# Re-cutting the last step's loads of a row-wise dot product: nine transfers become eight

## The chip, the cores and the metric

The kernel runs on one core of one Trainium2 chip. The time is that of the device for one execution, in microseconds (us). The kernel before takes 320.35 us, the median of three runs (320.31 to 320.41). The engines that matter here are VectorE (called DVE in the profile), ScalarE (ACT), SyncE (SP, which issues most transfers) and the core's 16 DMA engines. TensorE does no work.

## The reference

```
gram = np.matmul(x, y.transpose(0, 2, 1))          # x, y: (8, 4096, 512) float32
diag = np.diagonal(gram, axis1=1, axis2=2)         # (8, 4096)
diag = diag - diag.max(axis=-1, keepdims=True)
exp = np.exp(diag)
return exp / exp.sum(axis=-1, keepdims=True)
```

Only the diagonal of the product is used, so the work is 8 x 4096 dot products of a row of x with the same row of y, 512 long, and then a softmax over the 4096 values of each batch. Each input has 67.1 MB and is read once.

## The kernel before, in words

**Tiling.** Four batches at a time lie on the 128 partitions, 32 partitions to a batch, and each partition holds 128 consecutive rows of one batch (C = 128). The two groups of four batches are i = 0 and i = 1. A step `t` takes 32 of those 128 rows (R = 32) on all partitions, so there are eight steps, four to a group. A step's x is a tile of 128 x 32 x 512 (8.4 MB), its y as well. One "row" below means one row on every partition: 128 x 512 values, 256 KB.

**Buffers.** x has two buffers, `xs[0]` and `xs[1]`, used in turn. y has only one, `ys`. So the load of the next y must wait until the present y has been read. To let it go sooner, ScalarE copies a few rows of y elsewhere, so that VectorE may read these rows from the copy.

**Steps 0 to 5** (lines 123 to 134): load all 32 rows of x and of y, copy the last 6 rows of y to `side`, multiply on VectorE in two instructions (26 rows from `ys`, 6 from `side`, in place in `xs`, line 72), sum 30 rows on VectorE (line 75) and 2 rows on ScalarE (line 80).

**Step 6** (lines 136 to 146) has the same loads, but its y is cut at row F, which is H + 1 = 17. ScalarE copies the L = 9 rows of y that end at F into `spare`, which is rows 23 to 31 of `xs[1]`, the x buffer of step 7 (lines 139 and 140). VectorE multiplies the F - L = 8 rows ahead of these, then the 9 rows from `spare`, then the last 15 rows from `ys` (lines 141 to 143). After the first of the three and ScalarE's copy, rows 0 to 16 of `ys` are free. ScalarE sums 30 of the rows and VectorE 2.

**Step 7** (lines 149 to 161) loads x and y in nine pieces and takes them as they land. After each piece is issued, the rows that then have both x and y (`both`) are given to `dots`: one VectorE instruction a row, which multiplies and sums at once (line 85). The pieces are x 15, y 17, x 8, y 10, x 6, y 3, x 2, y 2, x 1 rows. When `both` reaches F, VectorE takes the largest of the values so far (line 161), 48 of them, and a later instruction on line 99 takes the largest of the remaining 18.

**The order of the work** is written by hand: each engine runs its instructions in program order and waits where a tile that it needs isn't ready. All loads and the first group's output transfers go through SP's queue in that order; an issue that waits holds up all issues behind it. A load waits for the instructions that last read or wrote its own rows of the buffer. The first y piece of step 7 (rows 0 to F - 1) thus waits for ScalarE's copy and VectorE's first product in step 6; the second y piece waits for the third product; an x piece that touches `spare` waits for the second product, which reads it.

**The end** (lines 163 to 169): eight small output transfers of the first group on SP, then the largest value, the exponential on ScalarE, the sum, the reciprocal, the scaling on VectorE, and the second group's output from ScalarE's queue.

Of the kernel before, what the change touches and what calls it, by code (L numbers as in the profile page):

```python
# [1 line left out]

# [5 lines left out]


@with_exitstack
def kernel(
    ctx: ExitStack,
    tc: tile.TileContext,
    x: bass.AP,
    y: bass.AP,
    out: bass.AP,
):
    nc = tc.nc
    ctx.enter_context(tc.manual_schedule())  # L20
    f32 = mybir.dt.float32
    Alu = mybir.AluOpType
    Act = mybir.ActivationFunctionType
    X = mybir.AxisListType.X
    B, N, D = x.shape
    P = nc.NUM_PARTITIONS
    G = 32
    Q = P // G
    C = N // G
    R = 32  # L30
    H = R // 2
    K = 6
    W = 2
    F = H + 1
    L = 9
    S = B // Q * (C // R)


    xv = x.rearrange("(s b) (j c) d -> s (b j) c d", b=Q, j=G)
    yv = y.rearrange("(s b) (j c) d -> s (b j) c d", b=Q, j=G)  # L40
    ov = out.rearrange("(s b) (j c) -> s (b j) c", b=Q, j=G)

    big = ctx.enter_context(tc.tile_pool(name="big", bufs=1))
    small = ctx.enter_context(tc.tile_pool(name="small", bufs=1))


    xs = [big.tile([P, R, D], f32, name=f"xs{i}") for i in range(2)]
    ys = big.tile([P, R, D], f32, name="ys")
    side = big.tile([P, K, D], f32, name="side")

    diag = [small.tile([P, C + 2 * i], f32, name=f"diag{i}") for i in range(B // Q)]
    res = [small.tile([P, C], f32, name=f"res{i}") for i in range(B // Q)]

    def columns(t, r0, n):
        c0 = t % (C // R) * R + r0
        return slice(c0, c0 + n)

    def rows(t, r0, n):
        return xs[t % 2][:, r0 : r0 + n, :]

    def dots_of(t, r0, n):
        return diag[t * R // C][:, columns(t, r0, n)]

    def load_x(t, r0, n):
        nc.sync.dma_start(out=rows(t, r0, n), in_=xv[t * R // C, :, columns(t, r0, n), :])  # L65

    def load_y(t, r0, n):
        nc.sync.dma_start(out=ys[:, r0 : r0 + n, :], in_=yv[t * R // C, :, columns(t, r0, n), :])  # L68

    def products(t, r0, n, yt):  # L70
        xt = rows(t, r0, n)
        nc.vector.tensor_tensor(out=xt, in0=xt, in1=yt, op=Alu.mult)  # L72

    def sums(t, r0, n):
        nc.vector.tensor_reduce(out=dots_of(t, r0, n), in_=rows(t, r0, n), axis=X, op=Alu.add)  # L75

    def sums_act(t, r0, n):
        for r in range(r0, r0 + n):
            row = xs[t % 2][:, r, :]
            nc.scalar.activation(out=row, in_=row, func=Act.Copy, accum_out=dots_of(t, r, 1))  # L80

    def dots(t, r0, n):
        for r in range(r0, r0 + n):
            xt = xs[t % 2][:, r, :]
            nc.vector.scalar_tensor_tensor(  # L85
                out=xt, in0=xt, scalar=1.0, in1=ys[:, r, :], op0=Alu.mult, op1=Alu.mult,
                accum_out=dots_of(t, r, 1),
            )

    def over_quadrant(name, column, op, negate=False):  # L90

        got = small.tile([P, 1], f32, name=name)
        nc.vector.tensor_reduce(  # L93
            out=got, in_=column.to_broadcast([P, G]), axis=X, op=op, negate=negate, apply_transpose=True
        )
        return got

    def largest(out, d):
        nc.vector.tensor_reduce(out=out, in_=d, axis=X, op=Alu.max)  # L99

    def exps(i, d):
        mxp = small.tile([P, 1], f32, name=f"mxp{i}")
        largest(mxp, d)
        nmx = over_quadrant(f"nmx{i}", mxp, Alu.max, negate=True)
        sump = small.tile([P, 1], f32, name=f"sump{i}")
        nc.scalar.activation(out=res[i], in_=diag[i][:, :C], func=Act.Exp, bias=nmx, scale=1.0, accum_out=sump)  # L106
        return sump

    def normalize(i, sump):
        total = over_quadrant(f"sum{i}", sump, Alu.add)  # L110
        rc = small.tile([P, 1], f32, name=f"rc{i}")
        nc.vector.reciprocal(out=rc, in_=total)  # L112
        nc.vector.tensor_single_scalar(out=res[i], in_=res[i], scalar=rc, op=Alu.mult)  # L113

    nc.vector.addr_align(128, offset=0, max_nops=0)
    nc.scalar.addr_align(128, offset=0, max_nops=0)

    nc.sync.drain()  # L120
    nc.sync.drain()  # L121

    for t in range(S - 2):
        load_x(t, 0, R)
        load_y(t, 0, R)
        nc.scalar.activation(out=side, in_=ys[:, R - K :, :], func=Act.Copy)  # L126
        if t == C // R:
            normalize(0, sump)
        products(t, 0, R - K, ys[:, : R - K, :])
        products(t, R - K, K, side)  # L130
        sums(t, 0, R - W)
        sums_act(t, R - W, W)
        if t == C // R - 1:
            sump = exps(0, diag[0])

    t = S - 2
    load_x(t, 0, R)
    load_y(t, 0, R)
    spare = rows(t + 1, R - L, L)
    nc.scalar.activation(out=spare, in_=ys[:, F - L : F, :], func=Act.Copy)  # L140
    products(t, 0, F - L, ys[:, : F - L, :])
    products(t, F - L, L, spare)
    products(t, F, R - F, ys[:, F:, :])
    sums(t, R - W, W)
    sums_act(t, 0, R - W)
    largest(diag[1][:, C + 1 :], diag[1][:, : C - 2 * R])


    t += 1
    upto = {load_x: 0, load_y: 0}  # L150
    done = 0
    for load, n in (
        (load_x, H - 1), (load_y, F), (load_x, 8), (load_y, 10), (load_x, 6), (load_y, 3), (load_x, 2), (load_y, 2), (load_x, 1)
    ):
        load(t, upto[load], n)
        upto[load] += n
        both = min(upto.values())
        dots(t, done, both - done)
        done = both
        if done == F:  # L160
            largest(diag[1][:, C : C + 1], diag[1][:, C - 2 * R : C - R + H])

    met = small.tile([P, C - R], f32, name="met")
    nc.scalar.activation(out=met, in_=diag[1][:, : C - R], func=Act.Copy)  # L164

    for p in range(0, P, H):
        nc.sync.dma_start(out=ov[0, p : p + H, :], in_=res[0][p : p + H, :])
    normalize(1, exps(1, diag[1][:, C - R + H :]))
    nc.scalar.dma_start(out=ov[1], in_=res[1])


# [1 line left out]
_INS = ['x', 'y']  # L173
_OUTS = [((8, 4096), 'float32')]


# [23 lines left out]
```

## Time and profile before

| what | value |
|---|---|
| median of three runs | 320.35 us (320.31 to 320.41) |
| profiled execution, first to last instruction (span) | 318.8 us |
| median less span | 1.55 us |
| VectorE busy | 241.7 us (76%) |
| ScalarE busy | 49.8 us (16%) |
| DMA moved | 134.37 MB, mean 421 GB/s |
| HBM read, written | 134.22 MB, 0.13 MB |

The span runs from the first to the last instruction of one profiled execution. The page gives no other time of that execution; what the measured median has above its span, 1.55 us, lies outside the instructions. Where the trace gives a transfer's "us to landing", it counts from the start of its issue on the queue to the time when all 16 DMA engines have reported it done. A share of DMA above 1 in a very short stretch only says that packets are booked at the moment when they begin. "issue" in the chain is time in which an engine waited for nothing that the profile shows.

### The profile page before, as it was taken

The page shows a single profiled execution, that of the slowest core. Times are in us where ns is not written, and L with a number is a line of the kernel's source. Part 1 is how long each engine was busy: PE and PEld are TensorE (multiplying, and loading weights), DVE is VectorE, ACT ScalarE, POOL GpSimd, SP SyncE. Part 2 cuts the span into 40 slices and gives each one's busy share as a digit, 9 for nine tenths or more (in the row PEclk, how much of TensorE's full clock was granted, in tenths as well). Part 3 has the DMA queues.
Part 4 walks back from the last instruction along what each step waited for, and adds up shares of the span by engine and source line. Part 5 has one row for each costly group of instructions (what it writes and reads, how often), then busy time and mean ns, then how long its engine had stood idle before and what let it go on. Part 6 is the DMA issues. An engine that isn't in the chain of part 4 may idle for free.

```text
span 318.8 us, 315 instructions
## 1 busy us (share of the span) xinstructions
DVE 241.7 (76%) x98; ACT 49.8 (16%) x97; POOL 0.2 (0%) x4
## 2 busy tenths in 40 slices
DVE  0000069995899939999399994999939998599996
ACT  1000030100301003010120103000030100596700
POOL 0000000000000000000000000000000000000000
DMA  9999999999999999999999999999999999999993
GB/s 372 419 395 469 452 395 452 469 395 395 493 428 395 469 452 395 428 477 411 395 485 436 395 469 452 395 403 493 419 395 469 452 395 452 394 440 410 429 411 112
DMA packets 3714, 134.37 MB, mean 421 GB/s; under 512 B 512, under 2 KB 768, under 8 KB 1280
## 3 DMA queue, kind: packets, MB, share of 16 engines
q1 hardware_dynamic: 3568, 134.29, 97.7%
q10 hardware_dynamic: 144, 0.07, 0.1%
q14 instruction: 2, 0.02, 0.0%
HBM read 134.22 MB, written 0.13 MB: 421 GB/s over the span
## 4 chain that ended last, share of the span: by engine, by line
DMA 65%; DVE 33%; SPq 1%; issue 0%; ACT 0%; DVEq 0%
DMA ys<-in_y_dram 65%; DVE xs L72 32%; DVE xs L85 0%; SPq L65 0%; SPq L68 0%; DVE res L113 0%; DVE sum L93 0%; DVE nmx L93 0%; ACT res L106 0%; DVE mxp L99 0%; DVE rc L112 0%; DVEq L72 0%; SPq L121 0%; SPq L120 0%
## 5 line engine op out<-in xcount | busy, mean ns | idle before, releaser
L72 DVE TENSOR_TENSOR xs<-xs,ys 128x13312 f32<-128x13312 f32 (+2 forms) x8 | 96.7, 12091 | 71.9 <-DMA ys<-in_y_dram 71.9
L75 DVE TENSOR_REDUCE diag<-xs 128x30 f32<-128x15360 f32 (+1 forms) x7 | 98.1, 14020 | 0.2
L80 ACT ACTIVATE xs<-xs 128x512 f32<-128x512 f32 x42 | 25.9, 617 | 90.4 <-DVE xs L72 90.4
L126 ACT ACTIVATE side<-ys 128x3072 f32<-128x3072 f32 x6 | 16.6, 2763 | 124.1 <-DMA ys<-in_y_dram 124.1
L85 DVE SCALAR_TENSOR_TENSOR xs<-xs,ys 128x512 f32<-128x512 f32 x32 | 19.9, 687 | 1.1 <-DMA ys<-in_y_dram 1.0
L72 DVE TENSOR_TENSOR xs<-xs,side 128x3072 f32<-128x3072 f32 x6 | 20.1, 3351 | 0.0
L80 ACT ACTIVATION_READ_ACCUMULATOR xs<-xs 128x1 f32 x42 | 7.9, 187 | 0.0
L140 ACT ACTIVATE xs<-ys 128x4608 f32<-128x4608 f32 x1 | 4.0, 4043 | 20.0 <-DMA ys<-in_y_dram 20.0
L106 ACT ACTIVATE res<-diag,nmx 128x128 f32<-128x128 f32 x2 | 0.8, 402 | 30.1 <-DVE nmx L93 30.1
L72 DVE TENSOR_TENSOR xs<-xs,xs 128x4608 f32<-128x4608 f32 x1 | 5.0, 4951 | 0.0
L85 DVE DVE_READ_ACCUMULATOR xs<-xs,ys 128x1 f32 x32 | 2.6, 82 | 0.0
L126 ACT ACT_TABLE_LOAD x1 | 1.3, 1283 | 1.2 <-PEq L184 1.2
L93 DVE TRANSPOSE_TENSOR_REDUCE sum<-sump 128x1 f32<-128x32 f32 x2 | 0.4, 212 | 1.2 <-ACT res L106 1.2
L113 DVE TENSOR_SCALAR res<-res,rc 128x128 f32<-128x128 f32 x2 | 0.6, 286 | 0.1
L99 DVE TENSOR_REDUCE mxp<-diag 128x1 f32<-128x128 f32 (+1 forms) x2 | 0.5, 229 | 0.1
L93 DVE TRANSPOSE_TENSOR_REDUCE nmx<-mxp 128x1 f32<-128x32 f32 x2 | 0.4, 211 | 0.1
L99 DVE TENSOR_REDUCE diag<-diag 128x1 f32<-128x64 f32 (+1 forms) x2 | 0.4, 202 | 0.0
L112 DVE RECIPROCAL rc<-sum 128x1 f32<-128x1 f32 x2 | 0.3, 164 | 0.1
L106 ACT ACTIVATION_READ_ACCUMULATOR res<-diag,nmx 128x1 f32 x2 | 0.4, 186 | 0.0
L164 ACT ACTIVATE met<-diag 128x96 f32<-128x96 f32 x1 | 0.3, 283 | 0.0
L184 POOL MEMSET const-bfloat16-1.0<- 128x1 bf16 x1 | 0.1, 102 | 0.0
L184 POOL MEMSET const-uint8-127<- 128x1 uint8 x1 | 0.1, 101 | 0.0
(2 smaller groups left out, 0.2 us busy)
## 6 DMA issues: line engine op xcount, KB each, us to landing
ys<-in_y_dram SPq DMA_DIRECT2D x1, 4352.0 KB, 14.9
xs<-in_x_dram SPq DMA_DIRECT2D x1, 3840.0 KB, 14.2
ys<-in_y_dram SPq DMA_DIRECT2D x1, 2560.0 KB, 12.9
xs<-in_x_dram SPq DMA_DIRECT2D x1, 2048.0 KB, 19.4
xs<-in_x_dram SPq DMA_DIRECT2D x1, 1536.0 KB, 16.3
ys<-in_y_dram SPq DMA_DIRECT2D x1, 768.0 KB, 17.7
xs<-in_x_dram SPq DMA_DIRECT2D x1, 512.0 KB, 18.5
ys<-in_y_dram SPq DMA_DIRECT2D x1, 512.0 KB, 19.3
```

What stands on the lines that cost most here:

```text
L72: nc.vector.tensor_tensor(out=xt, in0=xt, in1=yt, op=Alu.mult)
L75: nc.vector.tensor_reduce(out=dots_of(t, r0, n), in_=rows(t, r0, n), axis=X, op=Alu.add)
L80: nc.scalar.activation(out=row, in_=row, func=Act.Copy, accum_out=dots_of(t, r, 1))
L85: nc.vector.scalar_tensor_tensor(out=xt, in0=xt, scalar=1.0, in1=ys[:, r, :], op0=Alu.mult, op1=Alu.mult, accum_out=dots_of(t, r, 1),)
L93: nc.vector.tensor_reduce(out=got, in_=column.to_broadcast([P, G]), axis=X, op=op, negate=negate, apply_transpose=True)
L99: nc.vector.tensor_reduce(out=out, in_=d, axis=X, op=Alu.max)
L106: nc.scalar.activation(out=res[i], in_=diag[i][:, :C], func=Act.Exp, bias=nmx, scale=1.0, accum_out=sump)
L112: nc.vector.reciprocal(out=rc, in_=total)
L113: nc.vector.tensor_single_scalar(out=res[i], in_=res[i], scalar=rc, op=Alu.mult)
L126: nc.scalar.activation(out=side, in_=ys[:, R - K :, :], func=Act.Copy)
L140: nc.scalar.activation(out=spare, in_=ys[:, F - L : F, :], func=Act.Copy)
L164: nc.scalar.activation(out=met, in_=diag[1][:, : C - R], func=Act.Copy)
```

## The change

F becomes 20, so the cut of step 6's y moves from row 17 to row 20: VectorE's three products there have 11, 9 and 12 rows instead of 8, 9 and 15, and ScalarE's copy takes rows 11 to 19 of y instead of rows 8 to 16. The copy still goes to rows 23 to 31 of `xs[1]`. Step 7's pieces become x 13, y 20, x 12, y 8, x 5, y 3, x 2, y 1. The two `largest` calls of the second group split its values at F instead of at H = 16, so that the first takes 52 and the last 14.

```diff
-    F = H + 1
+    F = 20
...
     for load, n in (
-        (load_x, H - 1), (load_y, F), (load_x, 8), (load_y, 10), (load_x, 6), (load_y, 3), (load_x, 2), (load_y, 2), (load_x, 1)
+        (load_x, 13), (load_y, F), (load_x, 12), (load_y, 8), (load_x, 5), (load_y, 3), (load_x, 2), (load_y, 1)
     ):
...
         if done == F:
-            largest(diag[1][:, C : C + 1], diag[1][:, C - 2 * R : C - R + H])
+            largest(diag[1][:, C : C + 1], diag[1][:, C - 2 * R : C - R + F])
...
-    normalize(1, exps(1, diag[1][:, C - R + H :]))
+    normalize(1, exps(1, diag[1][:, C - R + F :]))
```

## The prediction

> **What bounds the kernel now.** I read the page first (who is busy, and the chain that ended last), then the chain in order of time, then the timeline and the DMA issues around steps 6 and 7, and last the stretches in which the DMA engines start and run dry.
>
> ```profile
> DVE 241.7 (76%) x98; ACT 49.8 (16%) x97; POOL 0.2 (0%) x4
> ...
> DMA  9999999999999999999999999999999999999993
> ...
> DMA 65%; DVE 33%; SPq 1%; issue 0%; ACT 0%; DVEq 0%
> ```
>
> The DMA row says 9 in all 39 slices ahead of the last: the engines never run dry until the end. The DVE share of the chain is VectorE giving the y buffer free, and behind it a load waits its turn in the queue anyway. So the span is the stream of loads plus a tail. The chain shows the tail:
>
> ```profile
> 274.78 17.37 DVE xs L72 x3
> ...
> 293.96 19.27 DMA ys<-in_y_dram
> 313.24 0.02 issue
> 313.26 1.40 DVE xs L85 x4
> 314.66 0.02 issue
> 314.68 0.18 DVE mxp L99
> ```
>
> After the last dot product 4.13 us follow (314.68 to 318.81: largest, exponential, sum, scaling, output), and the change leaves these as they are. The question is when line 99 can start. Two things run side by side up to there, the loads of step 7 and the dots on VectorE:
>
> ```profile
> 279.27 0.33 SPq L68 DMA_DIRECT2D ys<-in_y_dram  x1
> 279.64 0.43 SPq L65 DMA_DIRECT2D xs<-in_x_dram  x1
> ...
> 294.21 0.69 DVE L85 SCALAR_TENSOR_TENSOR xs<-xs,ys 128x512 f32<-128x512 f32 x1 [0.69 <-DMA ys<-in_y_dram]
> ...
> 304.63 0.20 DVE L99 TENSOR_REDUCE diag<-diag 128x1 f32<-128x48 f32 x1
> 305.13 0.69 DVE L85 SCALAR_TENSOR_TENSOR xs<-xs,ys 128x512 f32<-128x512 f32 x1 [0.30 <-DMA ys<-in_y_dram]
> ...
> 313.95 0.69 DVE L85 SCALAR_TENSOR_TENSOR xs<-xs,ys 128x512 f32<-128x512 f32 x1
> ```
>
> The first y piece is issued at 279.27, when VectorE's first product of step 6 ends. From 294.21 to 314.68 VectorE is nearly full too: 32 dots at 0.613 us from start to start are 19.62, the largest takes 0.20, and in all of 20.47 us only some 0.6 is idle. Loads and dots end almost together.
>
> ```profile
> ys<-in_y_dram SPq DMA_DIRECT2D x1, 4352.0 KB, 14.9
> xs<-in_x_dram SPq DMA_DIRECT2D x1, 3840.0 KB, 14.2
> ...
> xs<-in_x_dram SPq DMA_DIRECT2D x1, 256.0 KB, 19.5
> ```
>
> Issue plus landing gives when each piece is there: x15 at 269.63 + 14.2 = 283.83, y17 at 279.27 + 14.9 = 294.17, the last x1 at 294.44 + 19.5 = 313.94. The other issues of the trace give, by the same addition, x8 299.04, y10 305.07, x6 308.84, y3 310.72, x2 311.99, y2 313.26. Step 6's y landed at 250.21 + 24.48 = 274.69. One row costs b and one transfer a: y17 took 10.34 after x15 and x1 took 0.68 after y2, so b = (10.34 - 0.68) / 16 = 0.604 and a = 0.07. 64 rows and nine transfers make 39.29; measured are 313.94 - 274.69 = 39.25.
>
> **The change part by part.**
>
> *One transfer fewer.* The stream has the same 64 rows and eight times a: 0.07 less. The new landings, from 274.69: x13 282.61, y20 294.76, x12 302.08, y8 306.98, x5 310.07, y3 311.95, x2 313.23, y1 313.90. The issue that goes (0.43 on SP) lies 19 us ahead of its landing and is worth nothing.
> The Trainium skill ("DMA: Bandwidth & Descriptors", section on the anatomy of one DMA) puts a fixed 2.0 us on each DMA, for a path other than SP's; paid in line, the sum would be 2.0 lower by it. The small landings above, 0.68 apart, leave no room for that.
>
> *The dots start one row later.* They need the first x and y pieces, 33 rows now instead of 32. y20 lands at 294.76, and the first dot starts 0.04 behind it (as 294.21 behind 294.17): 294.80. From here I walk VectorE at 0.613 a dot: 13 dots to 302.77 (x12 there since 302.08), 7 to 307.06, the largest 0.22 to 307.28 (y8 since 306.98), 5 to 310.35 (x5 since 310.07), 3 to 312.19 (y3 since 311.95), 2 to 313.42 (x2 since 313.23), 1 to 314.03 (y1 since 313.90). So VectorE never waits, and the last dot starts at 314.03 instead of 313.95: +0.08. Each of the five group changes may cost the 0.02 seen at 308.81 to 308.83: I take +0.10 in all. If VectorE had no wait but the loads did decide, it would be 313.94 against 313.95, so no gain is in reach here. The 4 values more and fewer in the two largest calls are worth 196 - 208 = -12 ns for 16 values: 3 ns, nothing.
>
> *The first y piece is issued later.* VectorE's first product in step 6 has 11 rows instead of 8: 5632 values. 4096 took 4.42 and 13312 took 14.02, that is 1.042 ns each, so 5632 take 6.02 and end at 280.80 instead of 279.20. ScalarE's copy (274.79, 4.04, the same size) ends at 278.83 and is covered by it. With the same 0.07 from end to issue, y20 is issued at 280.87 (+1.60). At the same time x13 lands 1.22 earlier than x15 did. The lead of the issue over the end of the piece ahead shrinks from 283.83 - 279.27 = 4.56 us to 282.61 - 280.87 = 1.74 us. This is the one place where the stream can run dry, and nothing covers it: a gap g moves y20, every later piece and every dot by g.
>
> How long a lead an issue needs, the trace shows only at its two ends:
>
> ```profile
> 0.83 0.40 SPq L65 DMA_DIRECT2D xs<-in_x_dram  x1
> ...
> 1.50:1.75 0.25, 0.00 (x0) 0.25 (x1) 0.00 (x0) 1.00 0.00 0
> 1.75:2.00 0.25, 0.00 (x0) 0.25 (x1) 0.00 (x0) 1.00 4.22 1376
> ```
>
> The first load finds an empty queue. It is issued at 0.83 and its first packets begin between 1.75 and 2.00. x and y of step 0 (64 rows, two transfers: 38.80) are there at 1.28 + 41.12 = 42.40, so the empty start costs 42.40 - 0.83 - 38.80 = 2.77 us. That is the upper end: y20's data would start to count from 280.87 + 2.77 = 283.64 instead of 282.61, g = 1.03. But this start is cold: the third issue, at 1.75, took 1.24 us, where later ones took 0.33 to 0.43. The lower end is the last output, on a warm chip: 128 short rows issued on ScalarE's queue, there after 1.6 us in all, and the two SP outputs at the end after as little as 1.3. A need of 1.6 is under the lead of 1.74: g = 0. It can't be below nothing, as the pieces come in order. The engines don't end a piece together either, which softens the gap: at the very end the DMA share falls over a whole microsecond.
>
> ```profile
> 312.00:312.50 0.50, 0.50 (x1) 0.00 (x0) 0.00 (x0) 1.00 1.05 396
> 312.50:313.00 0.50, 0.50 (x3) 0.00 (x0) 0.00 (x0) 1.00 0.68 215
> 313.00:313.50 0.50, 0.44 (x3) 0.00 (x0) 0.00 (x0) 1.00 0.26 78
> 313.50:314.00 0.50, 0.50 (x3) 0.00 (x0) 0.00 (x0) 1.00 0.02 4
> ```
>
> A landing counts the last engine, and the first ones are done about 1 us before it. An engine that runs dry at 281.6 and starts again at 282.0 is still not later than the last one. So I take a need nearer to the warm row than to the cold one, 1.9 us, and g = 0.15.
> The Trainium skill (the same page, section on latency) gives about 600 ns to the first byte for SP's and ScalarE's DMAs; by it the new piece would begin at 281.47 and g would be 0. The first load's 0.92 to 1.17 us to its first packets is longer.
>
> *x12 now reaches into `spare`* (rows 13 to 24; the copy lies in rows 23 to 31), so it waits for VectorE's second product: 280.72 + 4.95 = 285.67. It is then issued at 285.7 instead of 279.64, and SP holds y8 and all issues behind it meanwhile. But its turn comes only at 294.76, 9 us later, and y8 has to wait for the third product until 292.1 anyway, as y10 did (292.17). Cost nothing; only if it were to be issued after 293 would it show.
>
> *Step 6's rest.* The three products keep 32 rows, so they end at 292.1 as before. ScalarE has 11 rows ready at 280.8 and then always enough: its 30 rows at 0.613 end at 299.3 instead of 300.25, and line 161, which reads them, comes at 307. The eight output issues wait for landings of loads, go behind them in the queue, and land by 315.4, under the tail.
>
> *Sum:* +0.10 (dots) + 0.15 (gap) = +0.25 on the span of 318.81, hence 319.06; with the 1.55 us that the median has above the span, 320.6.
>
> **The rivals.**
>
> *A, the gap is small (g up to 0.5)*: 320.4 to 320.95. For it: the warm row, and the spread of the engines. Chance 0.63.
>
> *B, slower: the stream runs dry between x13 and y20.* The mechanism is the lead of 1.74 us. If a start from an empty queue costs more than 2.25 us from issue, g is over 0.5 and the time over 320.99; with the cold start's 2.77, g is 1.03 and the time 320.35 + 0.10 + 1.03 = 321.5. For it: it is the only row of the same kind (128 rows, reads, SP's queue). Against it: it is the first thing that the chip does. Chance 0.33.
>
> *C, faster: the transfers in line cost more than I fitted.* To gain over 0.64 the stream would have to end 0.6 us sooner and VectorE lose its 0.6 us of idle time as well; but its walk above leaves it full from 294.80 on, and no earlier start is possible with 33 rows ahead. The one way would be that each transfer pays its own start in line: with the 1.3 us that the shortest output took from issue to landing, one transfer fewer gives 319.05. Against it: x1 landed 0.68 after y2, so less than that is paid for a transfer with its row. It is the rule of the page named above, with its 2.0 us in place of 1.3. Chance 0.04.
>
> **How the numbers follow.** 0.2% of 320.35 is 0.64 us, about what a measurement of this kernel tells from no change. A lies within it, B is slower, C faster. The likeliest is A with 320.6. The range must leave out no more than 2 in 10: the lower end is no gap and no cost at the group changes, less a little for the 0.07 saved, 320.3; the upper end takes in the cold start, 321.6. C and the far end of B are left out.
>
> **What the profile of the changed kernel would show.** The first y issue of step 7 at 280.87; landings at 282.6 for x13 and 294.76 + g for y20; the first dot at 294.80 + g; no idle time of VectorE from there to the last dot, which starts at 314.05 + g. With A the DMA row shows no dent near 282; with B a dent there, and all later pieces late by the same. The prediction is wrong if VectorE waits for a piece inside step 7, if x12 holds up the stream, or if g is above 0.5.

## The result and the profile after

The changed kernel takes 321.86 us (median of five runs, 321.57 to 322.57), against 320.41 us before (320.31 to 320.56, measured beside it). The ratio is 1.0049, with a 95% interval of 1.0038 to 1.0060: slower by 0.5%, or 1.45 us. The forecast was 320.6 with a range to 321.6, so the time lies outside the range, on the side of rival B.

The page of the changed kernel, parts 1, 2 and 4 (engines, the 40 slices, the chain that ended last):

```profile
DVE 241.5 (75%) x98; ACT 49.7 (16%) x97; POOL 0.2 (0%) x4
...
DMA  9999999999999999999999999999999999899992
...
DMA 63%; DVE 35%; issue 0%; SPq 0%; ACT 0%; DVEq 0%
```

The row of the DMA engines has an 8 in its 35th slice. A slice is 8.0 us, so this one covers 272 to 280 us and ends ahead of the gap found below; the slice that holds the gap shows a 9. Packets are booked where they begin, and a gap of 1 us in 8 us is too small for this row, so the dent that the prediction promised can't be read here. The chain in order of time says it better (start, length, what):

```profile
274.82 6.04 DVE xs L72
...
280.91 14.85 DMA ys<-in_y_dram
295.76 0.03 issue
295.79 0.02 DVEq L85
295.81 0.04 issue
295.85 12.35 DVE xs L85 x40
...
308.29 0.21 DVE diag L99
308.50 7.36 DVE xs L85 x24
315.86 0.02 issue
315.88 0.18 DVE mxp L99
```

Before, the chain went through the third product and the last y pieces. Now it leaves step 6 after the first product, passes through y20, and then VectorE's dots run to the end, with 0.09 us of rest ahead of the largest at 308.29. The issues and landings of the first two pieces (SP's timeline, then the DMA issues of the page):

```profile
269.63 0.33 SPq L65 DMA_DIRECT2D xs<-in_x_dram  x1
280.91 0.33 SPq L68 DMA_DIRECT2D ys<-in_y_dram  x1
285.74 0.33 SPq L65 DMA_DIRECT2D xs<-in_x_dram  x1
```

```profile
ys<-in_y_dram SPq DMA_DIRECT2D x1, 5120.0 KB, 14.9
xs<-in_x_dram SPq DMA_DIRECT2D x1, 3328.0 KB, 13.0
```

x13 lands at 269.63 + 13.0 = 282.63 and y20 at 280.91 + 14.85 = 295.76. Behind a fed queue 20 rows need 20 x 0.604 + 0.07 = 12.15 us, so the gap g is 295.76 - 282.63 - 12.15 = 0.98 us.

Where the time went can be read against the landing of step 6's y, which takes out what happened earlier in the execution. From there to the start of line 99 it was 314.68 - 274.69 = 39.99 us before and is 315.88 - (250.21 + 24.52) = 41.15 now: +1.16. Of this, 0.98 is the gap; the remaining 0.18 is the later start of the dots, for which the prediction had 0.10. The tail behind line 99 takes 4.19 us instead of 4.13, and step 6's y lands 0.04 later (274.73 instead of 274.69). Together these give the 1.26 us by which the traced span grew (318.81 to 320.07).

Two things make the median's +1.45 larger than the trace's. Each run of the experiments lists its time and its span, and these lie 1.73 to 1.83 us apart. The traced execution of before, with its span of 318.8, was thus one of about 320.6 us; most executions of before have a span of 318.4 to 318.7. And the gap isn't the same in each execution: the changed kernel's five spans go from 319.8 to 320.8, and the trace (320.1) is in the middle.

### The profile page after: what moved, and what is told of

The parts are those of the page before. It is cut to its first block, busy times and chain, and to the rows that moved or that the text cites. A ratio compares the mean times of both kernels' runs of the same rounds, so it can differ in the third digit from the quotient of the medians.

```text
span 320.1 us, 314 instructions
## 1 busy us (share of the span) xinstructions
DVE 241.5 (75%) x98; ACT 49.7 (16%) x97; POOL 0.2 (0%) x4
## 4 chain that ended last, share of the span: by engine, by line
DMA 63%; DVE 35%; issue 0%; SPq 0%; ACT 0%; DVEq 0%
DMA ys<-in_y_dram 63%; DVE xs L72 28%; DVE xs L85 6%; SPq L65 0%; DVE res L113 0%; DVE nmx L93 0%; DVE sum L93 0%; ACT res L106 0%; DVE diag L99 0%; DVE mxp L99 0%; DVE rc L112 0%; SPq L68 0%; DVEq L72 0%; DVEq L99 0%; DVEq L85 0%
## 5 line engine op out<-in xcount | busy, mean ns | idle before, releaser
L126 ACT ACTIVATE side<-ys 128x3072 f32<-128x3072 f32 x6 | 16.6, 2763 | 124.1 <-DMA ys<-in_y_dram 124.1
```

## The experiments

Three theories stood after the result. G: the loads run dry because y20 is issued too late ahead of x13's end, and a start from an empty queue costs 2.7 us from issue, as the first load of the kernel did. S: x12, which now touches the copy's rows, holds up the queue. T: the time comes from the larger pieces or from 33 rows ahead of the first dot. The number of rows that ScalarE copies (L) moves the lead alone: a longer copy leaves VectorE's first product shorter. "Lead" below is the landing of the first x piece less the issue of the first y piece. The four following ran on one chip, beside 13 runs of before (320.36).

**e1, a copy of 11 rows in the changed kernel**

```diff
-    L = 9
+    L = 11
```

> The changed kernel with a copy of 11 rows instead of 9, so that VectorE's first product of step 6 has 9 rows instead of 11; the eight pieces are unchanged. Theory G (the stream runs dry because y20 is issued only 1.7 us before x13 lands; a start from an empty queue needs 2.7 us from issue): the first product ends at 279.73, y20 is issued at 279.8, the lead is 2.8, no gap; y20 lands at 294.8 and the first dot starts there; time 320.5. Rival S (x12 now reaches into the copy's rows and holds up the queue) and rival T (the time comes from the larger pieces or from 33 rows ahead of the first dot): as the changed kernel, 321.5 to 322.

Measured: 321.63 (320.56 to 322.94, eight runs), ratio 1.0042 [1.0021, 1.0063]. The lead was as planned, and yet the traced execution shows the larger gap. SP's timeline, then the DMA issues:

```profile
269.37 0.33 SPq L65 DMA_DIRECT2D xs<-in_x_dram  x1
279.58 0.33 SPq L68 DMA_DIRECT2D ys<-in_y_dram  x1
```

```profile
ys<-in_y_dram SPq DMA_DIRECT2D x1, 5120.0 KB, 17.0
xs<-in_x_dram SPq DMA_DIRECT2D x1, 3328.0 KB, 13.0
```

y20 is issued 1.3 us sooner than in the changed kernel and takes 2.1 us longer: it lands at 296.6, with a gap of 2.10 us. The executions fall into two heaps, 320.56, 320.66, 320.82, 321.03 and 322.23, 322.71, 322.90, 322.94. So a lead of 2.79 us sometimes suffices and sometimes costs more than the shorter one. All three theories missed here: G, since its 2.7 us should have been enough, S and T, since half of the executions are nearly as fast as before, although x12's wait and the pieces are still there.

**e2, a copy of 10 rows**

```diff
-    L = 9
+    L = 10
```

> The changed kernel with a copy of 10 rows: the first product has 10 rows and ends at 280.27. Theory G: y20 is issued at 280.34, the lead is 2.27 and the gap 0.43, so y20 lands at 295.2 and the time lies between the others, 320.95. Rivals S and T: as the changed kernel, 321.5 to 322.

Measured: 323.12 (321.58 to 323.56), ratio 1.0079 [1.0063, 1.0095], the slowest of all. Lead 2.24 us, y20 lands 16.6 us behind its issue, gap 2.2 us. Against G's 0.43 that is five times too much, and S and T expected the changed kernel's time.

**e3, a copy of 7 rows**

```diff
-    L = 9
+    L = 7
```

> The changed kernel with a copy of 7 rows: the copy lies in rows 25 to 31 of the x buffer, so that x12 (rows 13 to 24) no longer touches it and need not wait for the second product; the first product has 13 rows. Theory G: y20 is issued at 281.94, the lead is 0.67, the gap 2.0; y20 lands at 296.8, time 322.6 to 323. Rival S: x12 is issued right behind y20 and the time goes back to 320.5. Rival T: as the changed kernel, 321.5 to 322.

Measured: 322.45 (322.20 to 322.89), ratio 1.0065 [1.0052, 1.0078]. SP's timeline of this run:

```profile
269.33 0.33 SPq L65 DMA_DIRECT2D xs<-in_x_dram  x1
281.68 0.33 SPq L68 DMA_DIRECT2D ys<-in_y_dram  x1
282.06 0.43 SPq L65 DMA_DIRECT2D xs<-in_x_dram  x1
```

x12 is issued right behind y20 and no longer waits, yet the kernel is slower than the changed one: S is out. The gap is 281.68 + 14.76 - 282.33 - 12.15 = 1.96 us, as G said (2.0); the median lies 0.15 below G's 322.6 to 323.

**e4, a copy of 4 rows in the kernel before**

```diff
-    L = 9
+    L = 4
```

> The kernel before, with its nine pieces, but with a copy of 4 rows instead of 9, so that the first product of step 6 has 13 rows instead of 8. Theory G: y17 is issued at 281.94 instead of 279.27, the lead over x15's landing at 283.83 falls to 1.9 and a gap of 0.8 opens; y17 lands at 295.0, time 321.2. Rivals S and T: the pieces are those of before, 320.4.

Measured: 321.85 (321.31 to 322.90), ratio 1.0051 [1.0036, 1.0065]. The nine pieces of before, issued later, cost as much as the change did. S and T can't give that: the pieces are those of before, and x8 is issued right behind y17, at 281.93. Lead 1.85 us, gap 1.1 us in the trace (G: 0.8); the median is 0.65 over G's 321.2.

The next four ran on another chip, beside 29 runs of before (320.41).

**e5, nothing that computes reads the rows that y20 overwrites**

```diff
-    nc.scalar.activation(out=spare, in_=ys[:, F - L : F, :], func=Act.Copy)
-    products(t, 0, F - L, ys[:, : F - L, :])
+    nc.scalar.activation(out=spare, in_=ys[:, F : F + L, :], func=Act.Copy)
+    products(t, 0, F - L, ys[:, F : 2 * F - L, :])
```

> The changed kernel, but step 6's first product and ScalarE's copy read other rows of y (rows 20 to 30 and 20 to 28 instead of 0 to 10 and 11 to 19), so that nothing that computes reads rows 0 to 19 of y; all instructions, their sizes and the eight pieces are the same, and 20 rows of step 6 get wrong values. y20 then waits only for step 6's y to land and is issued at about 274.8, 7.9 us ahead of x13's landing. If the short lead is the whole cause: y20 lands at 294.8 within 0.1, VectorE is full from there, time 320.45. If the larger pieces, the 33 rows ahead of the first dot or x12's wait for the second product cost something (all three are still there): what they cost stays, up to 321.8.

Measured: 320.69 (320.43 to 320.96, eleven runs), ratio 1.0006 [0.9997, 1.0015]. This is the decisive run: all instructions, the eight pieces, the 33 rows and x12's wait are those of the changed kernel, and only the lead differs (7.9 us). Its SP timeline, and its chain of waits from there on:

```profile
269.20 0.33 SPq L65 DMA_DIRECT2D xs<-in_x_dram  x1
274.31 0.33 SPq L68 DMA_DIRECT2D ys<-in_y_dram  x1
285.31 0.33 SPq L65 DMA_DIRECT2D xs<-in_x_dram  x1
```

```profile
274.31 20.02 DMA ys<-in_y_dram
294.34 0.03 issue
...
294.43 12.35 DVE xs L85 x40
...
314.46 0.18 DVE mxp L99
```

y20 lands at 294.33, which is 12.13 behind x13 (269.20 + 13.0): no gap. From the landing of step 6's y (249.78 + 24.51 = 274.29) to line 99 it is 40.17 us, 0.18 more than before: this is what the later start of the dots costs, and the rest of the changed kernel's 1.16 is the lead. In the packets of this trace, every engine goes from x13 to y20 without standing still, and all packets of y20 take 1.51 to 1.53 us, with the same work on VectorE and ScalarE beside them.

**e6, only the product reads other rows**

```diff
-    products(t, 0, F - L, ys[:, : F - L, :])
+    products(t, 0, F - L, ys[:, F : 2 * F - L, :])
```

> As the run before, but only the first product reads other rows of y (20 to 30), while ScalarE's copy reads rows 11 to 19 as in the changed kernel; 11 rows of step 6 get wrong values. y20 is issued when the copy ends, at 278.9, a lead of 3.7 us. If 2.7 us were enough on every DMA engine: 320.45. With the straggling of single engines seen at a lead of 2.8 (last first packet 4.2 us behind the issue): up to 0.5 more in some runs, 320.5 to 321.

Measured: 321.01 (320.58 to 321.23), ratio 1.0016 [1.0008, 1.0025]. Lead 3.73 us, gap 0.5 us in the trace. Two engines stand still, for 0.2 and 0.7 us, and the later one takes up y20 only 3.6 us behind the issue. So 3.7 us are still not quite enough.

**e7, the kernel before with x 13 ahead**

```diff
-        (load_x, H - 1), (load_y, F), (load_x, 8), (load_y, 10), (load_x, 6), ...
+        (load_x, H - 3), (load_y, F), (load_x, 10), (load_y, 10), (load_x, 6), ...
```

> The kernel before with x 13 ahead and x 10 as its second x piece instead of 15 and 8; the cut at row 17, the copy and all else as before. The first y piece is issued at 279.27 as before, but x13 lands at 282.6, so the lead is 3.3 instead of 4.6 us, and the first dot may start 1.2 us sooner. If the lead is enough: 320.35, the loads' end decides. If not: a spread from run to run between 320.4 and 322.

Measured: 320.81 (320.19 to 321.13, eleven runs), ratio 1.0007 [0.9999, 1.0016]. Two heaps again, 320.19 to 320.49 and 320.81 to 321.13. Lead 3.32, gap 0.44 in the trace, which is of the slower heap. In the faster one, a start of the dots 1.2 us sooner gains nothing over before that the runs can tell, since the loads' end decides.

**e8, the changed kernel again**

> The changed kernel again, beside the others on one chip: 321.9, with the gap of about 1.0 us at y20 that its first trace showed, if that gap comes each time; a spread of more than 1 us from run to run if the engines straggle by chance.

Measured: 321.84 (321.60 to 323.43), ratio 1.0055 [1.0039, 1.0072]. Gap 1.08 us in its trace, which is the fastest of its six executions; the slowest is 1.8 us above it. All eleven executions of the changed kernel, here and in the first comparison, are slower than every one of before beside them, and by how much differs from execution to execution.

The last two tested theory L, formed after e1 and e2: an issue that reaches engines still busy with the piece ahead gets to single engines later than one that finds them dry. They ran on a third chip, beside 17 runs of before (320.30).

**e9 and e10, copies of 6 and of 8 rows in the kernel before**

```diff
-    L = 9
+    L = 6    # e9
+    L = 8    # e10
```

> The kernel before with a copy of 6 rows instead of 9: the first product has 11 rows, y17 is issued 1.6 us later, and the lead over x15's landing falls from 4.6 to 3.0 us. Theory G (a start costs a fixed 2.7 us from issue): no gap, 320.4. Theory L (an issue that reaches engines still busy with the piece ahead gets to single engines only 3 to 4 us later, so that the worst leads are those of 2 to 3 us): a few engines run dry and start over 3 us behind the issue, a gap of up to 2 us in some executions and none in others, 320.4 to 322.9.

> The kernel before with a copy of 8 rows: the first product has 9 rows, y17 is issued 0.5 us later, the lead is 4.0 us. Theory G: no gap, 320.4. Theory L: the latest start seen is 4.2 us behind the issue, so hardly any gap: 320.4 to 320.7.

Measured: e9 321.83 (321.13 to 322.67), ratio 1.0046 [1.0035, 1.0057]; e10 320.40 (320.22 to 320.93), ratio 1.0003 [0.9994, 1.0011]. The pair differs by 1.0 us of lead and by 1.4 us of time. e9 decides against G, which expected 320.4. L expected some executions without a gap; all six were slower than every execution of before, so this part of L fails. e10 agrees with both, and in its trace no engine stands still between x15 and y17.

All runs by their lead; "need" is lead plus gap, that is the lead with which that execution would have had no gap. Gap and need are of the one traced execution, which was the fastest execution in e4, e8 and e9 and of the slower heap in e1 and e7:

| run | lead, us | gap in the trace, us | need, us | median less before's, us | executions, us |
|---|---|---|---|---|---|
| e3 | 0.65 | 1.96 | 2.6 | +2.09 | 322.20 to 322.89 |
| changed | 1.72 | 0.98 | 2.7 | +1.45 | 321.57 to 322.57 |
| e8 (changed) | 1.72 | 1.08 | 2.8 | +1.43 | 321.60 to 323.43 |
| e4 | 1.85 | 1.11 | 3.0 | +1.49 | 321.31 to 322.90 |
| e2 | 2.24 | 2.22 | 4.5 | +2.76 | 321.58 to 323.56 |
| e1 | 2.79 | 2.10 | 4.9 | +1.27 | 320.56 to 322.94 |
| e9 | 2.93 | 0.83 | 3.8 | +1.53 | 321.13 to 322.67 |
| e7 | 3.32 | 0.44 | 3.8 | +0.40 | 320.19 to 321.13 |
| e6 | 3.73 | 0.50 | 4.2 | +0.60 | 320.58 to 321.23 |
| e10 | 3.98 | 0.08 | | +0.10 | 320.22 to 320.93 |
| e5 | 7.89 | 0 | | +0.28 | 320.43 to 320.96 |

e5 and e10 show that the loads stay fed from a lead of about 4 us on; the kernel before has 4.56. Below that there isn't one price. With leads under 2 us the start takes 2.6 to 3.0 us, close to the 2.77 of the kernel's first load. With leads of 2.2 to 3.8 us it took 3.8 to 4.9 us in the traced executions. The differences of the medians hold more than the lead: e5 shows that the changed pieces cost 0.28 with no gap at all, so the changed kernel's lead costs 1.15 us (e8 less e5, beside the same runs of before).

The traces' single packets show how a start gets late. A piece comes in 128 packets, eight to each engine, and a landing counts the last engine. In the changed kernel the first packets of y20 begin on the 16 engines 1.0 to 2.0 us behind the issue. On average an engine stands still for 0.54 us between its last packet of x13 and its first of y20, and its eight packets of y20 take 12.66 us instead of e5's 12.14, as the first ones are slow. So about half of the gap is standing still and half is slow first packets. In e1 most engines take up y20 with hardly a pause, but three begin only 3.1 to 4.1 us behind the issue, after 1.0 to 2.6 us of standing still (the 4.2 of the expectations of e6 and e10 is 0.1 too much). In e2 two engines begin 3.0 and 3.1 us behind it.

## Why the prediction was wrong

*The place was right.* "This is the one place where the stream can run dry, and nothing covers it": e5 takes away only the short lead and gives back all but 0.3 of the 1.45 us. The issue at 280.87 came at 280.91, x13's landing at 282.61 came at 282.63.

*The step that failed is the size of the need:* "So I take a need nearer to the warm row than to the cold one, 1.9 us, and g = 0.15." It was 2.70 us in the changed kernel's trace and 2.80 in the second one, so the gap was 0.98 and 1.08 instead of 0.15. The row that was right is the cold one, the first load. The prediction had called it the only row of the same kind (a read of 128 rows on SP's queue), and set it aside because the chip had done nothing before. The warm row was an output of 128 packets of 512 bytes. Its first packet began 0.87 us behind the issue, hardly sooner than y20's first (0.95), but all 128 had begun 0.35 us later. What it lacks is what makes the cold row long: there the engines begin 1.0 to 2.5 us behind the issue, and their first packets of 64 KB take up to 3.2 us instead of 2.42. Both parts came back at y20.

*The softening failed too:* "An engine that runs dry at 281.6 and starts again at 282.0 is still not later than the last one." The engines don't start again together; their first packets are spread over 1.0 us and take 1.5 to 2.4 us instead of 1.51, so the last one lands as late as if it had waited for itself.

*The upper end was no end.* The cold start's 1.03 was taken as the largest gap. Executions of the changed kernel reached 323.43, 3.0 above before's median, and the table shows needs up to 4.9. The range's 321.6 therefore missed even the median. In the trace of before each load of steps 1 to 7 was issued at least 4.5 us ahead of the landing of the load before it, so it held no case of a late issue on a busy queue, and the spread of such a start could not be read there; a range with one such unknown should have gone further than the one row.

*The dots one row later:* +0.10 forecast, 0.18 measured (e5), and VectorE never waited for a piece from the first dot to the last, as walked. The largest in between added 0.31 to the time from one dot to the next, where the walk had 0.22. *The tail* was taken as unchanged; it takes some 0.06 more in each trace of the changed pieces. *x12 into the copy:* issued at 285.74 (forecast 285.7) and free of cost, by e3 and e5. *One transfer fewer:* in e5, with one transfer fewer and no gap, the last load lands 39.19 us behind step 6's y, where it was 39.24 before. The Trainium skill ("DMA: Bandwidth & Descriptors", anatomy of one DMA) states a fixed 2.0 us for each DMA of the path through GpSimd. This case has no load on that path; on SP's queue, once it is fed, no transfer pays as much in line: e5's last piece, of one row, landed 0.70 us behind the piece ahead.

*The baseline:* 1.55 us were taken as what lies around the span; by the runs that list both, it is about 1.79, and the traced execution of before was 0.2 us slower than most. This changed nothing in the difference.

*The first byte:* the earliest first packet of y20 begins 0.95 us behind its issue in the changed kernel, and none of the traces has an earlier one for this piece. The Trainium skill ("DMA: Bandwidth & Descriptors", section on latency) gives about 600 ns to the first byte for SP's DMAs; the trace does not agree. What the single late engines wait for, and why the first packets are slow, no run here shows. That stays open.

## What to carry to other kernels

Issue a load that has to wait for its buffer while enough of the earlier loads is still ahead of it; in this kernel leads of 4.0 and 4.6 us cost nothing that the runs can tell, and 1.7 us cost 1.15 us. When pieces are re-cut, compute this lead anew for the first piece that waits for something other than its turn: a smaller piece ahead of it and a larger piece behind it both shorten it. Price a start on a dry queue by the row of the same kind in the trace, here the kernel's first load, and let the range go beyond it.

## What the runs showed that was not expected

More lead can cost more: 2.2 us of lead gave +2.8 us, 1.7 us gave +1.4 us, with the same pieces. In the traces with leads of 2.2 to 3.8 us the last engine took up the piece 2.6 to 4.1 us behind its issue; with leads under 2 us it was 1.7 to 2.2 us. Theory L puts this down to engines that are still busy when the issue comes, but the changed kernel's engines were busy then too, so the reason isn't shown. The same kernel can have executions 2 us apart (e1: 320.56 and 322.94), while the runs of before on one chip lay within 0.75 us. A kernel whose loads run nearly dry thus shows itself by its spread as well as by its median.
